# Down projections of a decoder layer's two feed-forward blocks: features 8 to 21 by seven half-size products for each pair of output tiles

## The chip, the cores and the metric

The kernel runs on one core of one Trainium2 chip. The metric is the device time of one execution in microseconds (us). An engine is named as in the profile: PE is the matrix engine (TensorE), PEld its weight load, DVE the vector engine, ACT the scalar engine, POOL the GpSimd engine, SP the engine that mostly issues DMAs.

## The reference

One layer on 512 rows of 1024 values, all float32. The part that matters here is the feed-forward block, which stands at the start and at the end of the layer:

```python
D_FF = ((8 * D_MODEL // 3 + 127) // 128) * 128      # 2816 = 22 x 128

def swiglu(h, w_gate, w_up, w_down):
    return (jax.nn.silu(h @ w_gate) * (h @ w_up)) @ w_down

x = x + 0.5 * swiglu(rms_norm(x, norm_ffn1[l]), w1_gate[l], w1_up[l], w1_down[l])
# two token mixers, then the cross-attention
x = x + 0.5 * swiglu(rms_norm(x, norm_ffn2[l]), w2_gate[l], w2_up[l], w2_down[l])
return rms_norm(x, norm_final)
```

The change touches the last product of each block, `... @ w_down`: 2816 features in, 1024 values out, for 512 rows.

## The kernel before

The activations are held transposed: a tile has 128 features in its partitions and the 512 rows in its columns. So `x` is 8 tiles of 128x512, and the result of the gate and up projections, `act`, is 22 tiles of 128x512 ("features 0 to 21" below means these 22 tiles).

Every product in float32 is made of three matmuls in a format of less precision (`fp32r`). An operand `v` is split into `h` (ACT rounds it into `fp32r`) and `l = v - h` (DVE subtracts), and the product is `h*h + h*l + l*h`. `split` does this, and `wload` does it for a piece of weights: SP loads it (`wr`, three buffers), ACT writes `wh`, DVE writes `wl` (two buffers each).

The down projection of a block is the second half of the function `ffn`. It makes 8 output tiles. An output tile takes 22 features x 3 matmuls, each with a stationary 128x128 piece of weights and a moving 128x512 piece of `act`. The weights of an output tile come in three chunks of 8, 8 and 6 features (`DOWN`). The first two output tiles are computed together, chunk by chunk (line 553); tiles 2 to 7 go one after the other through `dense` (line 130). When a tile is done, DVE adds it to `x` (line 532), and `nrm.feed` adds its squares to the sum of the next norm (`acc`, line 188). In the second block the last tile is computed in two halves of 256 columns (again line 130), so that the end of the kernel (transposes, `finish`, line 1287; the output's scaling, lines 1305 and 1306; the output's DMAs, lines 1308 to 1311) can begin on the first half.

The gate and up projections ahead of it are already made by seven products of half-size blocks in place of eight: pairs of feature tiles, columns 0 to 255 and 256 to 511 as the two halves, with operand sums and result sums on DVE and ACT. Their recorded operations all have line 78. There a product has moving pieces of 128x256 or 128x512.

In the first block a `hook` makes tables for the mixers between the tiles of the down projection: at tile 3 four small matmuls (line 644) make a position table from a one-hot matrix `oh`, DVE copies them out (`fab`, line 646), POOL sends them to DRAM (line 647), and POOL then issues 16 DMAs that spread them (line 651).

The order on each engine comes from a scheduler with priorities, save where `ordered()` or `high_priority` holds an instruction. An engine runs its instructions in that order, and each waits for what it reads and for the buffer that it writes.

## Time and profile before

| | us |
|---|---|
| time, median of 3 runs | 1260.16 (1260.11 to 1261.1) |
| the profiled execution: time | 1260.48 |
| the profiled execution: span from first to last instruction | 1258.5 |
| down projection of the first block, on PE | 232.40 to 357.98 |
| down projection of the second block, on PE | 1121.89 to 1249.65 |

The span is the time between the first and the last instruction in the trace, so 1.98 us of the profiled time lie outside it. "Busy" sums overlapping instructions only once. Matmuls are pipelined: one shows a duration of 0.28 or 0.39 us, but the next starts sooner, and what counts is the distance between starts (the pitch). All positions are microseconds from the start of the span.

### The profile page before, as it was taken

What the parts mean: (1) busy time and instruction counts of PE and PEld (TensorE: products, weight loads), DVE (VectorE), ACT (ScalarE), POOL (GpSimd) and SP (SyncE); (2) the same over time, 40 slices, a digit from 0 to 9 for tenths busy, and PEclk for the clock granted to TensorE, in tenths of its full rate; (3) what the DMA queues carried; (4) which work ended last, traced back from release to release, by engine and by line L of the source; (5) the groups of instructions that cost most, each with busy time, mean ns of one, the idle gap of its engine ahead of it and who ended that gap; (6) DMA issues with size and microseconds to landing.
All of it is one profiled execution on the core that took longest, in us unless ns stands there. A gap on an engine that the chain in (4) does not pass through costs nothing.

```text
span 1258.5 us, 17814 instructions
## 1 busy us (share of the span) xinstructions
PE 1247.4 (99%) x6517; PEld 1052.5 (84%) x6517; DVE 895.6 (71%) x1842; ACT 704.7 (56%) x1424; POOL 74.8 (6%) x101
## 2 busy tenths in 40 slices
PE   9999999999999999999999999999999999999997
PEld 7888888887888788888888898887888888888887
DVE  5899888844356988887878666555689888884224
ACT  5466666732244777777774554444547666672223
POOL 1001111003000000000001000000001111000000
PEclk9999999999999999999999999999999999999999
DMA  6738776238443522221224345212446777723233
GB/s 222 192 101 192 194 188 175 79 117 257 149 139 101 184 66 96 71 77 55 84 89 156 112 134 184 84 51 67 124 136 175 192 193 179 182 73 104 84 101 113
DMA packets 58791, 165.93 MB, mean 132 GB/s; under 512 B 6248, under 2 KB 6512, under 8 KB 58704
## 3 DMA queue, kind: packets, MB, share of 16 engines
q1 hardware_dynamic: 44096, 129.16, 32.0%
q0 software_dynamic: 14032, 34.57, 12.8%
q8 instruction: 51, 0.84, 0.3%
q10 hardware_dynamic: 576, 1.07, 0.2%
q14 instruction: 36, 0.29, 0.1%
HBM read 160.54 MB, written 10.07 MB: 136 GB/s over the span
## 4 chain that ended last, share of the span: by engine, by line
PE 95%; DVE 3%; ACT 1%; DMA 1%; issue 0%; DVEq 0%; SPq 0%; ACTq 0%
PE ps_d L130 44%; PE ps_d L78 12%; PE ps_t L78 8%; PE ps_d L553 5%; PE ps_s L78 5%; PE ps_o L78 4%; PE ps_d L1044 4%; PE ps_d L1198 2%; PE ps_t L929 1%; PE ps_s L842 1%; PE ps_o L837 1%; PE ps_s L841 1%; PE ps_o L836 1%; PE ps_d L792 1%; PE ps_o L1257 1%; PE ps_s L1231 1%
## 5 line engine op out<-in xcount | busy, mean ns | idle before, releaser
L105 ACT ACTIVATE wh<-wr 128x512 fp32r<-128x512 f32 (+3 forms) x255 | 167.5, 690 | 302.2 <-PE ps_d L130 160.0
L106 DVE TENSOR_TENSOR wl<-wr,wh 128x512 fp32r<-128x512 f32 (+3 forms) x255 | 189.6, 769 | 142.1 <-ACT wh L105 140.2
L130 PE MATMUL ps_d<-xh,wl 128*128 128x512 f32 x424 | 169.8, 400 | 0.0
L130 PE MATMUL ps_d<-xh,wh 128*128 128x512 f32 x424 | 168.6, 398 | 0.0
L130 PE MATMUL ps_d<-xl,wh 128*128 128x512 f32 x424 | 168.4, 397 | 0.0
L130 PEld LDWEIGHTS ps_d<-xh,wl 128*128 128x128 f32 x424 | 79.7, 188 | 16.5 <-DVE wl L106 0.5
L130 PEld LDWEIGHTS ps_d<-xl,wh 128*128 128x128 f32 x424 | 79.7, 188 | 15.9
L130 PEld LDWEIGHTS ps_d<-xh,wh 128*128 128x128 f32 x424 | 79.8, 188 | 15.6
L130 PE MATMUL ps_d<-al,wh 128*128 128x512 f32 (+1 forms) x195 | 73.9, 379 | 0.0
L130 PE MATMUL ps_d<-ah,wh 128*128 128x512 f32 (+1 forms) x195 | 73.9, 379 | 0.0
L130 PE MATMUL ps_d<-ah,wl 128*128 128x512 f32 (+1 forms) x195 | 73.8, 378 | 0.0
L78 DVE TENSOR_TENSOR wl<-wr,wh 128x1024 fp32r<-128x1024 f32 (+1 forms) x49 | 52.1, 1071 | 20.9 <-ACT wh L78 20.8
L130 PE MATMUL ps_d<-ahl,wh 128*128 128x512 f32 (+1 forms) x182 | 53.1, 376 | 0.0
L78 PE MATMUL ps_o<-t,h2h 128*128 128x256 f32 x272 | 50.4, 283 | 0.0
L78 DVE TENSOR_TENSOR h2l<-s,h2h 128x512 fp32r<-128x512 f32 x68 | 44.1, 688 | 8.4 <-ACT h2h L78 8.0
L78 PE MATMUL ps_d<-n,h2h 128*128 128x512 f32 x136 | 49.9, 401 | 0.0
L78 PE MATMUL ps_d<-t,h4h 128*128 128x512 f32 x136 | 49.6, 399 | 0.0
L78 PE MATMUL ps_t<-b,h5h 128*128 128x512 f32 x136 | 49.4, 397 | 0.0
L78 PE MATMUL ps_t<-n,h3h 128*128 128x512 f32 x136 | 49.3, 395 | 0.0
L78 PE MATMUL ps_s<-b,wh 128*128 128x512 f32 x136 | 49.1, 395 | 0.0
L78 PE MATMUL ps_d<-b,wh 128*128 128x512 f32 x136 | 49.0, 393 | 0.0
L78 ACT ACTIVATE wh<-wr 128x1024 fp32r<-128x1024 f32 (+1 forms) x49 | 45.2, 931 | 6.8 <-DMA wr<-in_w_first_dram 3.6
(387 smaller groups left out, 3306.3 us busy)
## 6 DMA issues: line engine op xcount, KB each, us to landing
wr<-in_w_down_dram SPq DMA_DIRECT2D x34, 512.0 KB, 3.5
wr<-in_w_in_dram SPq DMA_DIRECT2D x29, 512.0 KB, 3.5
wr<-in_w_gate_dram SPq DMA_DIRECT2D x25, 512.0 KB, 4.9
wr<-in_w_up_dram SPq DMA_DIRECT2D x25, 512.0 KB, 5.1
s<-in_w_gate_dram SPq DMA_DIRECT2D x17, 512.0 KB, 4.5
s<-in_w_gate_dram POOLq DMA_DIRECT2D x17, 512.0 KB, 6.0
s<-in_w_up_dram SPq DMA_DIRECT2D x17, 512.0 KB, 4.2
s<-in_w_up_dram POOLq DMA_DIRECT2D x17, 512.0 KB, 6.5
```

The lines of the kernel that those rows point to most:

```text
L78: return lambda *args, **kw: tc.keep_in_program_order(call(*args, **kw))
L105: A.activation(h, src, AF.Copy)
L106: V.tensor_sub(l, src, f32(h))
L130: yield T.matmul(out, w[:, c], m, start=i == 0, stop=i == total - 1)
L553: T.matmul(two[m], w[:, cc], v, start=f == 0 and z == 0, stop=f == FT - 1 and z == 2)
L792: T.matmul(pv[i][:, :VC], m[k][:, tk], ww[:, w], start=k == 0 and z == 0, stop=k == KT - 1 and z == 2)
L836: T.matmul(po[:, cols], w, h[:, src], start=start, stop=False, skip_group_check=True)
L837: T.matmul(po[:, cols], w, l[:, src], start=False, stop=False, skip_group_check=True)
L841: first = T.matmul(out, q[:, tk], kk[0][:, ks], start=True, stop=False)
L842: T.matmul(out, q[:, tk], kk[1][:, ks], start=False, stop=True)
L1044: yield T.matmul(pj, w[:, c], m, start=n == 0, stop=n == 11)
L1198: T.matmul(pj[t], m[k][:, tk], ww[:, w], start=k == 0 and z == 0, stop=k == KT - 1 and z == 2)
```

## The change

`ffn` is cut into `gate_up` and `down`, with memory pools of their own. In `down`, features 0 to 7 (`NA`) are multiplied as before, for all 8 output tiles. Features 8 to 21 are taken as two halves, 8 to 14 and 15 to 21 (`ND` = 7 tiles each). With two output tiles and the two halves of the columns, this is a product of 2x2 blocks, and it is made by seven products of blocks in place of eight, for each of four pairs of output tiles. One product is 7 features x 3 matmuls with a moving piece of 128x256.

The sums of blocks of `act` (`nt`, `nt2`) and their splits (`b11`, `nh` and `nl`, `bh` and `bl`) are made by `prepare_top` and `prepare_bottom`; the sums of blocks of the weights are made by a DMA that adds (`load_s`: SP loads one half twice, POOL adds the other) and by DVE (`s2`). `ready(i)` makes the weights of product `i`, two products ahead. `results` copies a partial sum on ACT or adds a finished one to `x` on DVE, 256 columns at a time. The tables are made ahead of tile 4 in place of tile 3 (`HOOK` = 3, called with `m - 1`), in four pieces, in buffers shared with the block operands. The end of the second block is written anew for the new order of its results (`part`, `turn`, `sums`, `leave`), with as many transposes and output DMAs as before. The diff, cut to its core:

```diff
-DOWN = (8, 8, 6)
+NA = 8
+ND = (FT - NA) // 2
+WD = ND * P
+NK = 22
...
+HOOK = 3
+BOTTOM = {0: (2,), 1: (3, 4), 2: (5, 6)}
+TOPS = (2, 1, 1, 1, 1, 1)
...
-                    ahead.append(down_weights(q + 1 - NQ, 0))
+                    ahead.append(wload(a[f"w{tag}_down"][q + 1 - NQ][:, :NA * P], NA * P))
...
+        def load_s(q):
+            q_[q]["s"] = t = pool.tile([P, 2, WD], F32, tag="S", name="s31", bufs=2)
+            o = src[2 * q + 1]
+            SY.dma_start(t, bass.AP(o.tensor, o.offset + NA * P, [[FF, P], [0, 2], [1, WD]]))
+            o = src[2 * q]
+            G.dma_start(t, bass.AP(o.tensor, o.offset + NA * P, [[FF, P], [P * FF + WD, 2], [1, WD]]),
+                        accum_op=ALU.add)
...
+        def prepare_top(k):
+            t, b = act[NA + k], act[NA + ND + k]
+            ta, tb_, ba, bb = t[:, :256], t[:, 256:], b[:, :256], b[:, 256:]
+            nt, nt2 = ext("nt"), ext("nt2")
+            V.tensor_sub(nt[:, :256], ta, tb_)
+            V.tensor_sub(nt[:, 256:], bb, tb_)
+            V.scalar_tensor_tensor(nt2[:, :256], nt[:, :256], -1.0, bb, op0=ALU.mult, op1=ALU.subtract)
+            V.scalar_tensor_tensor(nt2[:, 256:], nt2[:, :256], -1.0, ba, op0=ALU.mult, op1=ALU.subtract)
+            b11 = block("b11")
+            blk["b11"][k] = b11[:, :256], b11[:, 256:]
+            split(*blk["b11"][k], ta)
+            for n1, n2, v in (("n1", "t3", nt), ("n2", "t4", nt2)):
+                h, l = block("nh"), block("nl")
+                split(h, l, v)
+                blk[n1][k] = h[:, :256], l[:, :256]
+                blk[n2][k] = h[:, 256:], l[:, 256:]
+
+        def prepare_bottom(k):
+            h, l = block("bh"), block("bl")
+            split(h, l, act[NA + ND + k])
+            blk["b21"][k] = h[:, :256], l[:, :256]
+            blk["b22"][k] = h[:, 256:], l[:, 256:]
...
+        for f in range(NA):
+            if ah[f] is None:
+                act_split(f)
...
+        seq = []
+        NQ = KT // 2
+        for q in range(NQ):
+            seq += [("1", q), ("7", q)]
+            if q:
+                seq.append(("4", q - 1))
+            if last and q == NQ - 1:
+                seq += [("6", q), ("2", q), ("4", q), ("3", q - 1), ("5", q), ("3", q)]
+                break
+            seq += [("6", q), ("2", q)]
+            if q:
+                seq.append(("3", q - 1))
+            seq.append(("5", q))
+            if q == NQ - 1:
+                seq += [("4", q), ("3", q)]
+        used = {"1": "b11", "7": "t3", "6": "n2", "2": "b21", "5": "n1", "4": "t4", "3": "b22"}
+        def ready(i):
...
+            if p == "7":
+                d["s2"] = pool.tile([P, WD], F32, tag="s2", name="s2", bufs=2)
+                V.tensor_add(d["s2"], d["s"][:, 1], d["r11"])
+            raw = {"1": "r11", "2": "r12", "4": "r22", "3": "s2", "6": "s2"}.get(p)
+            raw = d[raw] if raw else d["s"][:, 0 if p == "7" else 1]
+            if last and i == len(seq) - 1:
+                t = pool.tile([P, 2, WD], F32R, tag="S", name="ws", bufs=2)
+                ws[i] = t[:, 0], t[:, 1]
+            elif i % 3 == 1:
+                ws[i] = tuple(pool.tile([P, WD], F32R, tag="w3" + z, name="w3", bufs=1) for z in "hl")
+            else:
+                ws[i] = tuple(t[:, :WD] for t in wpair())
+            split(*ws[i], raw)
+            if p == ("2" if last and q == NQ - 1 else "5"):
+                V.tensor_add(d["s2"], d["s2"], d["r12"])
+            n = {"7": "r11", "5": "r12", "4": "r22"}.get(p)
+            if n and q + 1 < NQ:
+                load(q + 1, n)
+            if p == "5" and q + 2 < NQ:
+                load_s(q + 2)
+        tops = list(range(ND))
+        for m in range(2, KT):
+            if hook:
+                hook(m - 1)
+            pd = bank("d")
+            dense(pd, [(src[m][:, :NA * P], NA)], ah, al, step=1024)
+            if m < KT - 1:
+                update(m, pd)
+            else:
+                with ordered():
+                    for n in ("r11", "r12", "r22"):
+                        load(0, n)
+                    with tc.high_priority(offset=AHEADF):
+                        ready(0)
+                        ready(1)
+                    update(m, pd)
+            for _ in range(TOPS[m - 2]):
+                prepare_top(tops.pop(0))
+        for k in range(2):
+            prepare_bottom(k)
+
+        def product(out, w, n, start=False):
+            for k in range(ND):
+                c = slice(k * P, (k + 1) * P)
+                h, l = blk[n][k]
+                for i, (ww, m) in enumerate(((w[0], h), (w[0], l), (w[1], h))):
+                    T.matmul(out, ww[:, c], m, start=start and k + i == 0, stop=k == ND - 1 and i == 2,
+                             skip_group_check=True)
...
+        def results(i):
...
+            if p == "1":
+                d["ga"] = bank("s")
+                A.activation(d["ga"][:, :256], d["x"][:, :256], AF.Copy)
+            elif p == "6":
+                d["gb"] = bank("t")
+                A.activation(d["gb"][:, :256], d["x"][:, :256], AF.Copy)
+            elif p == "7":
+                late.append(lambda: add7(m + 1, d["p7"]))
+            elif p == "2":
+                add(m, 0, d["ga"], 1)
...
+        def seven():
...
+                d = q_[q]
+                for k in BOTTOM.get(i, ()):
+                    prepare_bottom(k)
+                if not (last and i == len(seq) - 3):
+                    ready(i + 2)
...
+            for n in "sstt":
+                t = bank(n)
+                T.matmul(t[:, :256], ah[0][:, :P], al[0][:, :256], start=True, stop=True, skip_group_check=True)
+            seven()
...
-        TB = ((0, 1024, "h2h"), (1024, FA + FB - 1024, "h2l"))
+        TB = ((0, 512), (512, 512), (1024, FA - 1024), (FA, FB))
...
-            if m != 3:
+                return
+            if m != HOOK:
                 return
...
-                        fab = pool.tile([P, S], F32, tag="E", name="fab", bufs=NE)
-                        V.tensor_copy(fab[:8, :e1 - e0], b[:8, :e1 - e0])
-                        nc.gpsimd.dma_start(dst[:, e0 - lo:e1 - lo], fab[:8, :e1 - e0])
...
+                fab = pool.tile([P, S], F32, tag="E", name="fab", bufs=4)
+                V.tensor_copy(fab[:8, :n], b[:8, :n])
+                nc.gpsimd.dma_start(dst[:, c0 - lo:c0 - lo + n], fab[:8, :n])
```

How the order of instructions changes is shown at two places. First PE in the first block. Before, in the middle of an output tile (here tile 4, `ps_d`), features 0 to 7 (`ah`, `al`) were followed by features 8 and on (`ahl`):

```order
L130 MATMUL ps_d_3060<-ah_2704,wh_3093 128x512
L130 MATMUL ps_d_3060<-al_2705,wh_3093 128x512
L130 MATMUL ps_d_3060<-ah_2704,wl_3094 128x512
L130 MATMUL ps_d_3060<-ahl_2708,wh_3093 128x512 x2
L130 MATMUL ps_d_3060<-ahl_2708,wl_3094 128x512
L130 MATMUL ps_d_3060<-ahl_2775,wh_3123 128x512 x2
L130 MATMUL ps_d_3060<-ahl_2775,wl_3124 128x512
```

Now all 8 output tiles end with feature 7; after the last (tile 7) come four matmuls into unused banks, and then the first two of 28 products (operands `b11` and `nh`, `nl`; weights `wh`, `wl` and `w3`):

```order
L136 MATMUL ps_d_2990<-ah_2624,wh_2993 128x512
L136 MATMUL ps_d_2990<-al_2625,wh_2993 128x512
L136 MATMUL ps_d_2990<-ah_2624,wl_2994 128x512
L84 MATMUL ps_s_3065<-al_841,ah_840 128x256
L84 MATMUL ps_s_3067<-al_841,ah_840 128x256
L84 MATMUL ps_t_3069<-al_841,ah_840 128x256
L84 MATMUL ps_t_3071<-al_841,ah_840 128x256
L84 MATMUL ps_d_3081<-b11_2718,wh_3027 128x256 x2
L84 MATMUL ps_d_3081<-b11_2718,wl_3028 128x256
```

In place of 42 matmuls of 512 columns for features 8 to 21 in each tile, PE has 147 matmuls of 256 columns for each pair of tiles, behind all the others.

The second place is DVE in the same block. Before, between the additions of two finished tiles to `x` (tiles 4 and 5), it had the splits of three chunks of weights (`wl`), one step of the norm and one split for the next stage (`xl`):

```order
L532 SCALAR_TENSOR_TENSOR x4_65<-ps_d_3060,x4_65 128x512
L106 TENSOR_TENSOR wl_3183<-wr_3180,wh_3182 128x1024
L188 TENSOR_TENSOR acc_2832<-acc_2832,sq_3146 128x512
L234 SCALAR_TENSOR_TENSOR xl4_3433<-x4_65,gains_69,xh4_3432 128x512
L106 TENSOR_TENSOR wl_3213<-wr_3210,wh_3212 128x768
L106 TENSOR_TENSOR wl_3242<-wr_3239,wh_3241 128x1024
L532 SCALAR_TENSOR_TENSOR x5_66<-ps_d_3149,x5_66 128x512
```

Now, from the addition of the last tile on (`x7`, features 0 to 7 only), the splits of block operands stand between the splits of weights; `wl_3078` is for the third product (number 6), `wl_3114` for the fourth, `w3_3148` for the fifth:

```order
L84 SCALAR_TENSOR_TENSOR x7_68<-ps_d_2990,x7_68 128x512
L112 TENSOR_TENSOR nl_3054<-nt2_3041,nh_3053 128x512
L112 TENSOR_TENSOR bl_3058<-act_1901,bh_3057 128x512
L112 TENSOR_TENSOR bl_3062<-act_2091,bh_3061 128x512
L84 TENSOR_TENSOR bl_3074<-act_2129,bh_3073 128x512
L84 TENSOR_TENSOR wl_3078<-s2_3031,wh_3077 128x896
L84 TENSOR_TENSOR bl_3106<-act_2316,bh_3105 128x512
L84 TENSOR_TENSOR bl_3110<-act_2354,bh_3109 128x512
L84 TENSOR_TENSOR wl_3114<-wr_3023,wh_3113 128x896
L84 TENSOR_TENSOR bl_3140<-act_2520,bh_3139 128x512
L84 TENSOR_TENSOR bl_3144<-act_2555,bh_3143 128x512
L84 TENSOR_TENSOR w3_3148<-s31_2606,w3_3147 128x896
```

The norm's steps and the splits `xl` have moved behind, into the products; the work on block operands is new at this place.

## Rows read from the trace of the kernel before

**Rows 1.** The page: the span, the busy time of the engines (share of the span, number of instructions), and the shares of the chain of work that ended last.

```profile
span 1258.5 us, 17814 instructions
...
PE 1247.4 (99%) x6517; PEld 1052.5 (84%) x6517; DVE 895.6 (71%) x1842; ACT 704.7 (56%) x1424; POOL 74.8 (6%) x101
...
PE 95%; DVE 3%; ACT 1%; DMA 1%; issue 0%; DVEq 0%; SPq 0%; ACTq 0%
```

**Rows 2.** Windows: start and end of a stretch and its length; then PE, PEld, DVE, ACT and POOL busy (number of instructions); the granted clock of PE, the DMAs' share and GB/s. The stretches are the end of the gate and up projections of the first block, two parts of its down projection, the gate and up projections of the second block, and two parts of its down projection.

```profile
76.00:232.40 156.40, 156.32 (x951) 139.39 (x952) 139.18 (x252) 108.10 (x210) 16.46 (x15) 1.00 0.67 175
232.40:279.00 46.60, 46.60 (x204) 37.40 (x203) 25.44 (x42) 19.47 (x34) 1.10 (x2) 1.00 0.33 102
279.00:358.00 79.00, 79.00 (x341) 62.98 (x340) 28.98 (x37) 20.92 (x28) 13.05 (x25) 1.00 0.59 189
...
945.00:1122.00 177.00, 176.80 (x1072) 157.31 (x1073) 157.14 (x283) 119.61 (x234) 17.70 (x15) 1.00 0.67 171
1122.00:1167.00 45.00, 45.00 (x198) 36.43 (x197) 23.58 (x40) 19.40 (x34) 0.00 (x0) 1.00 0.31 94
1167.00:1249.80 82.80, 82.80 (x441) 70.63 (x440) 29.34 (x43) 25.96 (x38) 0.00 (x0) 1.00 0.31 98
```

**Rows 3.** Timeline of PE at the start and the end of the first block's down projection, and at the start of the second's: start, duration, operation, output from inputs, shape.

```profile
232.40 0.39 PE L553 MATMUL ps_d<-ah,wh 128*128 128x512 f32 x1
...
357.98 0.40 PE L130 MATMUL ps_d<-xh,wh 128*128 128x512 f32 x1
...
1121.89 0.39 PE L553 MATMUL ps_d<-ah,wh 128*128 128x512 f32 x1
```

**Rows 4.** The chain of waits, in order of time: start, length, what, and the number of instructions in the piece. The first is a product of the gate and up projections with 256 columns; the others are pieces of the down projections, the second of them the leftover of the stage before.

```profile
104.45 1.44 PE ps_o L78 x12
...
233.72 1.55 PE ps_t L78 x8
...
286.27 74.67 PE ps_d L130 x320
...
1242.34 7.47 PE ps_d L130 x62
```

**Rows 5.** Timeline of PE in the last output tile of the second block: the first matmul of its first half (66 matmuls of 256 columns), the last, and the transposes behind.

```profile
1232.20 0.28 PE L130 MATMUL ps_d<-ah,wh 128*128 128x256 f32 x1
...
1239.91 0.28 PE L130 MATMUL ps_d<-ahl,wl 128*128 128x256 f32 x1
1240.04 0.82 PE L1287 MATMUL ps_d<-ident,gx 128*128 128x128 f32 x6
```

**Rows 6.** Groups of instructions of one line and shape, from 1228 to 1250 us: PE's weight loads for matmuls of 256 columns: number, busy us, mean ns of one, idle us before them.

```profile
L130 PEld LDWEIGHTS ps_d<-ah,wh 128*128 128x128 f32 x30 | 5.7, 188 | 0.0
```

**Rows 7.** The same view for DVE and ACT: four shapes on DVE over the whole span, the addition to `x` and a 256-column operation between 76 and 360 us, and two shapes on ACT.

```profile
L106 DVE TENSOR_TENSOR wl<-wr,wh 128x1024 fp32r<-128x1024 f32 x38 | 46.5, 1225 | 49.2 <-ACT wh L105 49.1
L106 DVE TENSOR_TENSOR wl<-wr,wh 128x768 fp32r<-128x768 f32 x11 | 10.5, 958 | 35.2 <-ACT wh L105 35.2
L532 DVE SCALAR_TENSOR_TENSOR x<-ps_d,x 128x512 f32<-128x512 f32 x8 | 5.5, 692 | 16.9 <-PE ps_d L130 13.0 <-PE ps_d L553 3.9
L78 DVE TENSOR_TENSOR act<-act,sg 128x256 f32<-128x256 f32 x16 | 6.8, 425 | 0.5
L105 ACT ACTIVATE wh<-wr 128x512 fp32r<-128x512 f32 x196 | 114.6, 623 | 148.1 <-PE ps_d L130 74.2 <-issue 27.2 <-PE ps_d L553 19.8
L105 ACT ACTIVATE wh<-wr 128x1024 fp32r<-128x1024 f32 x38 | 40.3, 1060 | 114.5 <-PE ps_d L130 82.5 <-issue 20.6 <-PE ps_d L553 6.4
```

**Rows 8.** Timeline of DVE at the start of the first block's down projection, for the distance between starts: 256 columns (the first three), 512 columns (the last two).

```profile
232.60 0.42 DVE L78 TENSOR_TENSOR act<-ps_t,p 128x256 f32<-128x256 f32 x1
233.06 0.42 DVE L78 TENSOR_TENSOR act<-ps_t,act 128x256 f32<-128x256 f32 x1
233.40 0.41 DVE L78 TENSOR_TENSOR act<-ps_d,p 128x256 f32<-128x256 f32 x1
...
238.33 0.69 DVE L106 TENSOR_TENSOR al<-act,ah 128x512 fp32r<-128x512 f32 x1
238.93 0.69 DVE L106 TENSOR_TENSOR ahl<-act,ahl 128x512 fp32r<-128x512 f32 x1
```

**Rows 9.** DMA issues: number, KB each, median us from issue to landing.

```profile
wr<-in_w_down_dram SPq DMA_DIRECT2D x34, 512.0 KB, 3.5
s<-in_w_gate_dram SPq DMA_DIRECT2D x17, 512.0 KB, 4.5
s<-in_w_gate_dram POOLq DMA_DIRECT2D x17, 512.0 KB, 6.0
s<-in_w_up_dram POOLq DMA_DIRECT2D x17, 512.0 KB, 6.5
fa_r<-fa_d POOLq DMA_DIRECT2D x8, 520.0 KB, 11.9
fa_d<-fab POOLq DMA_DIRECT2D x2, 16.0 KB, 2.7
```

**Rows 10.** Timeline of the end of the kernel: the last matmul, the addition of the last half tile to `x`, and the first scaling of the last output rows.

```profile
1249.53 0.28 PE L130 MATMUL ps_d<-ahl,wl 128*128 128x256 f32 x1
...
1249.85 0.42 DVE L565 SCALAR_TENSOR_TENSOR x<-ps_d,x 128x256 f32<-128x256 f32 x1 [2.06 <-PE ps_d L130]
...
1252.64 0.69 ACT L1305 ACTIVATE out<-ps_o,nr 128x512 f32<-128x512 f32 x1 [0.82 <-DVE nr L214]
```

## The prediction

> **What bounds the kernel now.** I read the page first: of a span of 1258.5 us PE is busy for 1247.4, and the chain of work that ended last is PE for 95% [rows 1]. The reader is to see that the time is a count of matmuls times their pitch. Then the windows by stage: in both down projections PE is busy in every microsecond at a granted clock of 1.00, while DVE is busy 25.4 of the first 46.6 us and 29.0 of the next 79 us of the first block, and much the same in the second [rows 2]. So in these two stages a matmul less is time less, as long as DVE, ACT and the DMAs keep up; and DVE has room, though not without end: in the gate and up projections it is busy 139.4 of 156.4 us, and PE still has no gap there [rows 2]. The down projection of the first block runs on PE from 232.40 to 357.98 us, where the next stage's first matmul starts without a gap [rows 3]: 125.6 us. The second's runs from 1121.89 us [rows 3] to the last matmul's end at 1249.53 + 0.12 = 1249.65 us [rows 10]: 127.8 us.

> **The pitches.** A matmul of 512 columns: 320 of them in 74.67 us of the chain, 0.2333 us each [rows 4]. A matmul of 256 columns: 12 in 1.44 us, 0.120 [rows 4]; 66 without any other between 1232.20 and 1240.04 us, 0.1188 [rows 5]; 62 in 7.47 us at the end, 0.1205, among a few others [rows 4]. I take 0.1195 with ends of 0.1188 and 0.1205. Half the columns cost 0.512 of the whole, so the seven-for-eight saving survives nearly unhurt.

> The rule that speaks against this: each of these matmuls has a weight load of its own, which shows 188 ns [rows 6], more than the pitch of 120 ns, but it lies beside other matmuls and weight loads, since 66 in a row kept 0.1188. [...]

> **The change, part by part.** Removed, in each block: features 8 to 21, that is 8 tiles x 14 x 3 = 336 matmuls of 512 columns. Added: 4 pairs x 7 products x 7 x 3 = 588 matmuls of 256, and 4 more into unused banks.

> First block: 336 x 0.2333 = 78.39 us go, 592 x 0.1195 = 70.74 come: -7.65 us. The four small table matmuls stay, and so does the leftover of the stage before, 1.55 us [rows 4]. Second block: there the last tile already ran in halves. 7 tiles x 42 = 294 matmuls of 512 go, and 84 of 256. The pitch of 512 is a little shorter in this block: from 1121.89 to 1232.20 us [rows 3, 5] lie 462 of them, the leftover of about 1.5 us and 16 transposes of about 0.12, which gives (110.3 - 1.5 - 1.9)/462 = 0.2314. So 68.0 + 84 x 0.1195 = 78.1 go, 70.7 come, and the first features of the last tile go back from 48 x 0.1195 to 24 x 0.2314 (-0.2): -7.5 us. Together -15.2 us. The ends of the narrow pitch move this by 1184 x 0.0007 = 0.8 down or 1184 x 0.001 = 1.2 up.

> Behind the last matmul nothing should change: adding the last half tile to `x` starts 0.3 us after it began, and the first output scaling 2.8 us later [rows 10]; the new end has the same half tile, sums, transposes and output DMAs. I cost it at 0, from -0.5 to +1.5: before, 66 matmuls (7.9 us) [rows 5] and more lay between the ends of the two halves of the rows, now one product (2.5 us), so the output DMAs of the first half lie closer to those of the second.

> What must be hidden is DVE's and ACT's work in the first 46 us, and this is where I expect a small loss. PE takes 192 x 0.2333 + about 2.5 us (leftover and tables) + 0.5 from 232.40 until the products start: 280.2 us. The first three products (2.5 us each) put the start of the third, number 6, at 285.2. DVE must by then have done 76 instructions, counted in its new order from 238.93 us, where before it began the splits of features 8 and on [rows 8]. Of 256 columns: 28 sums of blocks and 7 splits, at a pitch of 0.34 where the operands are old [rows 8] and up to 0.43, a whole duration [rows 7], where each waits for the one before (21 can): 35 x 0.34 = 11.9 to 13.8. Of 512: 17 splits at 0.60 [rows 8], 10.2, and 8 additions to `x` at 0.60 to 0.69 [rows 7], 5.2. Of 1024: 6 splits at 1.225 [rows 7] less the 0.09 by which neighbours overlap, 6.8. Of 896 columns, which this trace doesn't have: 4, between 0.958 and 1.225 [rows 7], nearer the latter, 1.09 less 0.09: 4.0. The tables: 1.7. Sum 39.8 to 41.7, so ready at 279 to 281 if DVE never waits. But it runs in order, and two waits stand in the way: the addition of tile 3 stands ahead of the table copies and waits for PE (some 2 us), and the next sum of blocks (`nt`) takes the buffer of a table copy whose DMA needs 2.7 us to land [rows 9] (some 1 to 2). That gives 282 to 285 against 285.2. The margin is 0 to 3 us. Queued behind these waits are the splits of weights for tiles 5 to 7 and the first products, and PE waits for those. I take a loss of 0.8 us for the first block, from 0 to 5. In the second there are no tables, and I take 0, up to 2.

> ACT has 14 `nh`, 7 `b11`, 3 `bh` and 4 splits of weights more in that stretch: 17 x 0.62 + 7 x 0.40 + 4 x 0.95 = 17 us beside the 19.5 it has, less the splits of features 8 to 21 that go: below 37 of 47 us [rows 2, 7]. It hides.

> In the products a pair lasts 147 x 0.1195 = 17.6 us. DVE has 7 splits and 2 sums of 896 (9 x 1.0), one addition of 512 and four of 256 (0.7 + 4 x 0.4), two norm steps (2 x 0.6) and, in the first block, two splits for the next stage (2 x 0.7): about 13.9 us, 79%, where the gate and up projections run 89% [rows 2]. The weights of a product are split two products ahead, 5 us, against about 2.0 for one split on ACT and DVE. A pair's weights are 3.2 MB of reads, 182 GB/s; the gate and up stages move 171 to 175 without a gap on PE [rows 2]. The adding DMA takes 6.0 to 6.5 us to land [rows 9] and is issued more than a pair ahead; in the first block it shares POOL's queue with the 16 table DMAs, which land in 11.9 us [rows 9]. I cost this at 0, from 0 to 3.

> Sum against the profiled execution: 1260.48 - 15.2 + 0.8 = 1246.1; that execution is 0.3 us above the median. I predict 1246 us. Its own range is 1243.8 to 1249.

> **The rivals.**

> *PE waits at the joint.* DVE's queue is late by more than the margin in the first block, and a little in the second, so that PE stands still ahead of the first products: 3 to 9 us together. For it: the waits above, and a stage that goes from 55% DVE [rows 2] to about 95%. Against it: PE's gap-free gate and up stage at 89%. Time 1249 to 1255, point 1251. Chance 0.18.

> *Products held by their own operands (slower).* Place: every product. If the lead of two products is used up by DVE's in-order queue (an addition to `x` that waits for PE stands ahead of a split that PE waits for), each product waits for its split. 56 products lose the gain of 15.2 us when each waits 0.27; half of a 896 split on DVE (0.55 us) each is 56 x 0.55 = 31 us, 1276. For it: 9 splits and sums in line with 5 additions per pair. Against: 21% of DVE's time free and 5 us of lead. Chance 0.07.

> *The gain is given back, no change.* The adding DMAs come late behind the table DMAs, one pair waits for a landing of 12 us in the first block, and the end gains nothing: about 1260. That the gate and up stages move 171 to 175 GB/s with adding DMAs of the same kind and no gap [rows 2, 9] is against it. Chance 0.03.

> *Narrow matmuls paced by their weight loads (slower).* At 0.188 us [rows 6] for each of 1176 the change costs 1176 x 0.188 - 2 x 78.3 = +65 us, 1325; it decides from a pitch of 156.5/1176 = 0.133. The 66 in a row at 0.1188 speak against it [rows 5]. [...] Chance 0.02.

> **How the numbers follow.** The forecast's own range gets 0.67; 0.03 is left for below 1243.8, if the narrow pitch is at its low end and nothing waits. The range of 8 in 10 takes in the joint's waits: 1243.5 to 1254. About 0.2% (2.5 us) is what a measurement of this kernel can tell from no change. Faster: 0.67 + 0.18 + 0.03 = 0.88; same 0.03; slower 0.07 + 0.02 = 0.09.

> **What would show it.** The products' rows should have a pitch of 0.119 to 0.121 us, and each block's down projection should last 118 to 120 us on PE. If I am right about the joint, idle time ahead of PE's weight loads is below 2 us, released by DVE `wl` or `w3` around product 6 of the first block. Steps gone wrong would be: idle time of PE ahead of every product (second rival), a releaser among DMAs in the first block (third), a pitch above 0.125 (last), or more than 10 us between the last matmul's start and the span's end.

## The result, and the profile after

The change takes 1245.7 us (median of 4 runs, 1245.47 to 1246.24) against 1260.6 us (median of 4, 1260.11 to 1261.1) before: a ratio of 0.9882 with a 95% interval of 0.9865 to 0.99. That is 14.9 us less, and the spans of the profiled executions differ by as much, 1258.5 and 1243.6.

The page after, its span, engines and chain, as in [rows 1]:

```profile
span 1243.6 us, 18977 instructions
...
PE 1232.5 (99%) x6979; PEld 1066.1 (86%) x6979; DVE 978.5 (79%) x1990; ACT 740.0 (60%) x1478; POOL 85.6 (7%) x111
...
PE 95%; DVE 3%; ACT 1%; DMA 1%; issue 0%; ACTq 0%; SPq 0%; DVEq 0%
```

PE has 462 instructions more and 14.9 us less of work, DVE 83 us more, and the bound is still PE. The windows by stage, as in [rows 2] (stretch, length, PE, PEld, DVE, ACT, POOL, clock, DMA share, GB/s): first part and products of the first block, gate and up projections and what lies around them, first part and products of the second block.

```profile
232.40:280.00 47.60, 47.60 (x211) 38.06 (x210) 43.22 (x85) 24.24 (x43) 15.58 (x27) 1.00 0.83 260
280.00:349.30 69.30, 69.30 (x591) 69.30 (x590) 56.47 (x76) 39.29 (x57) 7.95 (x12) 1.00 0.66 190
349.30:1113.10 763.80, 761.39 (x4061) 645.77 (x4060) 586.87 (x1323) 466.68 (x1014) 37.54 (x47) 1.00 0.41 121
1113.10:1159.80 46.70, 46.70 (x206) 37.67 (x205) 43.36 (x83) 26.02 (x42) 2.36 (x2) 1.00 0.59 169
1159.80:1234.10 74.30, 74.30 (x631) 74.30 (x630) 51.66 (x74) 37.66 (x56) 2.36 (x2) 1.00 0.38 106
```

PE has no gap in any of the four stretches that the change touches, at a granted clock of 1.00. DVE in the first 47 us went from 25.4 to 43.2 us of work [rows 2], and still nothing waits. The timeline of PE gives the bounds of the stages, as in [rows 3]:

```profile
232.50 0.39 PE L606 MATMUL ps_d<-ah,wh 128*128 128x512 f32 x1
...
279.96 0.40 PE L84 MATMUL ps_d<-b,wh 128*128 128x256 f32 x2
...
349.28 0.39 PE L136 MATMUL ps_d<-xh,wh 128*128 128x512 f32 x1
...
1112.90 0.39 PE L606 MATMUL ps_d<-ah,wh 128*128 128x512 f32 x1
```

| us | before | after | difference | predicted |
|---|---|---|---|---|
| down projection, first block | 125.58 | 116.78 | -8.8 | -6.85 |
| between the two | 763.91 | 763.62 | -0.3 | 0 |
| down projection, second block | 127.76 | 121.23 | -6.5 | -7.5 |
| last matmul's start to the end | 8.97 | 9.59 | +0.6 | 0 |

At the joint, the timelines of PE and of its weight loads, and of DVE, around product 6:

```profile
284.80 0.29 PE L84 MATMUL ps_o<-nh,w 128*128 128x256 f32 x1
284.92 0.28 PE L84 MATMUL ps_d<-nh,wh 128*128 128x256 f32 x1
```

```profile
285.04 0.19 PEld L84 LDWEIGHTS ps_d<-nh,wl 128*128 128x128 f32 x1
```

```profile
282.10 0.69 DVE L84 TENSOR_TENSOR bl<-act,bh 128x512 fp32r<-128x512 f32 x1
282.70 1.08 DVE L84 TENSOR_TENSOR wl<-s,wh 128x896 fp32r<-128x896 f32 x1
```

Product 6 starts at 284.92. Its `wl` is finished at 282.70 + 1.08 = 283.78 and first loaded at 285.04: a margin of 1.3 us.

### The profile page after: what moved, and what is told of

Read it like the earlier page. It is cut to its first block, busy times and chain, and to the rows that moved or that the text cites. A ratio compares the mean times of both kernels' runs of the same rounds, so it can differ in the third digit from the quotient of the medians.

```text
span 1243.6 us, 18977 instructions
## 1 busy us (share of the span) xinstructions
PE 1232.5 (99%) x6979; PEld 1066.1 (86%) x6979; DVE 978.5 (79%) x1990; ACT 740.0 (60%) x1478; POOL 85.6 (7%) x111
## 4 chain that ended last, share of the span: by engine, by line
PE 95%; DVE 3%; ACT 1%; DMA 1%; issue 0%; ACTq 0%; SPq 0%; DVEq 0%
PE ps_d L136 36%; PE ps_d L84 17%; PE ps_t L84 11%; PE ps_s L84 6%; PE ps_o L84 6%; PE ps_d L1306 4%; PE ps_d L1460 2%; PE ps_d L606 2%; PE ps_t L1191 1%; PE ps_s L1104 1%; PE ps_o L1099 1%; PE ps_s L1103 1%; PE ps_o L1098 1%; PE ps_d L1054 1%; PE ps_o L1519 1%; PE ps_s L1493 1%
## 5 line engine op out<-in xcount | busy, mean ns | idle before, releaser
L111 ACT ACTIVATE wh<-wr 128x512 fp32r<-128x512 f32 (+1 forms) x206 | 132.7, 679 | 151.4 <-PE ps_d L136 69.6
L112 DVE TENSOR_TENSOR wl<-wr,wh 128x512 fp32r<-128x512 f32 (+1 forms) x206 | 150.0, 754 | 31.8 <-ACT wh L111 29.8
L136 PEld LDWEIGHTS ps_d<-xh,wl 128*128 128x128 f32 x424 | 79.8, 188 | 16.5 <-DVE wl L112 0.5
L84 DVE TENSOR_TENSOR wl<-wr,wh 128x1024 fp32r<-128x1024 f32 (+2 forms) x67 | 71.7, 1075 | 24.6 <-ACT wh L84 24.2
L84 ACT ACTIVATE wh<-wr 128x1024 fp32r<-128x1024 f32 (+2 forms) x67 | 62.3, 935 | 17.7 <-PE ps_o L84 4.6
L84 PE MATMUL ps_d<-b,wh 128*128 128x512 f32 (+1 forms) x220 | 64.2, 351 | 0.0
L84 DVE TENSOR_TENSOR s<-s,wr 128x512 f32<-128x512 f32 (+1 forms) x84 | 63.9, 760 | 0.0
L84 PE MATMUL ps_d<-b,wl 128*128 128x256 f32 x178 | 50.1, 281 | 0.6 <-DVE wl L84 0.6
L84 POOL DMA_DIRECT2D s<-in_w_gate_dram x17 | 20.1, 1182 | 357.2 <-DMA s<-in_w_gate_dram 286.6
L84 ACT ACTIVATE h2h<-s 128x512 fp32r<-128x512 f32 x68 | 39.1, 623 | 8.8 <-DVE s L84 8.8
```

The source lines that it names most:

```text
L84: return lambda *args, **kw: tc.keep_in_program_order(call(*args, **kw))
L111: A.activation(h, src, AF.Copy)
L112: V.tensor_sub(l, src, f32(h))
L136: yield T.matmul(out, w[:, c], m, start=i == 0, stop=i == total - 1)
```

## Experiments

**One block alone.** The second block's down projection and the end are those of before (the old function, called for that block):

```diff
+    def ffn_old(pool, tag, nrm_in, gin, nrm, gi, first=None, hook=None, done=None):
```

> The first block as changed, the second block's down projection and end as before. My theory (matmul count times pitch, block by block): the trace of the change has the first block's down projection 8.8 us shorter and the second's 6.5 us shorter with an end 0.6 us longer, so this kernel should be 8.8 us faster than before, about 1251.8, with 0.3 either way. Rival (part of the gain lies in the second block's new end or in the split of the pools, not in the products): the first block alone would give clearly less, 7 us or below.

Measured: 1252.2 us (1251.99 to 1252.32), ratio 0.9933 (0.9916 to 0.9949). The first block's stage lasts 116.78 us as in the change, the second's 127.75 as before. So the first block's gain does not need the second's change. It is 8.8 us by the stage and 8.5 by the time (the end came out 0.4 us longer here): larger than the 6.85 I had forecast for it, with the second's smaller.

**The lead of the operands.** `ready(i)` makes the weights of product i on ACT and DVE; the change calls it two products ahead.

```diff
-                        ready(1)
...
-                if not (last and i == len(seq) - 3):
-                    ready(i + 2)
-                if last and i == len(seq) - 5:
-                    ready(i + 4)
+                ready(i + 1)
```

> As changed, but the weights of a product are made one product ahead, not two. My theory: a split takes about 2.0 us on ACT and DVE (3.0 with a sum ahead of it) against 2.5 us for a product, so some products now wait a few tenths: +2 to +10 us, and the idle time of PE is released by DVE wl or w3. Rival (products are never near to waiting, the lead is worthless): 0 within 1 us. Rival (even now each product is held by its operands): +50 us or more.

With `ready(i)` right ahead of the product instead:

> As changed, but the weights of a product are made right ahead of it in the program's order, behind the addition of the product before on DVE. My theory: where such an addition stands ahead (some 40 of 56 products), PE waits for the addition (0.4), the split on DVE (1.0) and where there is one the sum (1.0): 1.5 to 2.5 us each, +60 to +100 us. Rival (the order of DVE does not matter since it has 20% of its time free): below +10 us.

Measured, one run each: 1249.9 us with a lead of one (4.2 above the change; the first stage 1.3 and the second 2.3 us longer), and 1361.2 with none (115 above it; the stages 46 and 65 us longer). The second figure is beyond what I expected. The windows of the products without a lead:

```profile
279.90:392.00 112.10, 76.98 (x550) 70.56 (x548) 54.14 (x70) 35.46 (x51) 7.41 (x11) 0.95 0.40 111
1208.00:1347.00 139.00, 97.26 (x631) 89.62 (x630) 55.07 (x76) 38.20 (x57) 2.36 (x2) 0.87 0.23 64
```

PE stands idle for 35 of 112 us and 42 of 139, and the granted clock has a mean of 0.95 and 0.87. Part of the matmuls are slower too: from 288.35 to 291.12 us they start 0.213 us apart in place of 0.118. How the excess divides between waiting and slower matmuls was not measured apart. A product that waits for its own operands loses 46/28 = 1.6 us in the first block, the slower matmuls included, not the 0.55 that my second rival gave it. The lead of two is what keeps that rival out; one product is nearly enough.

**Narrow matmuls.** The second block's products as two matmuls of 128 columns, 1176 of them:

```diff
+                    for z in ((0, 128, 256) if last else (0, 256)), :
+                        for z0, z1 in zip(z, z[1:]):
+                            T.matmul(out[:, z0:z1], ww[:, c], m[:, z0:z1], start=start and k + i + z0 == 0,
```

> As changed, but in the second block each matmul of a product is made as two of 128 columns, 1176 in place of 588. If columns alone set the pitch (half of 0.119 us each), nothing changes: 0 to +2 us. If a matmul cannot come sooner than its weight load allows, the transposes of 128 columns in the traces (0.109 us from start to start) are the floor: 1176 x 0.109 = 128 us in place of 70, +58 us. I lean to the second: 256 columns would then lie just above the floor.

Measured, in one run: 1307.1 us, 61.4 above the change. Two pieces of the chain of waits of this kernel (start, length, what, instructions), and the row of one group of its weight loads (number, busy us, mean ns of one, idle us before them):

```profile
1174.10 4.69 PE ps_s L84 x42
...
1192.86 9.38 PE ps_d L84 x84
```

```profile
L84 PEld LDWEIGHTS ps_d<-nh,wl 128*128 128x128 f32 x84 | 12.8, 192 | 0.0
```

Half the columns again cost 0.1117 us, not 0.06. The 192 ns that a weight load lasts are not the pace, since a matmul with one of its own follows every 112 ns. The sums of squares at the end of the change, of a single column, come every 0.111 us (8 in 0.89 us, in the rows further down). So 256 columns at 0.118, 128 at 0.1117 and one at 0.111 us lie close together. Why was not tested; the weight loads, one for each matmul, come at the same distance (from 1160 to 1296 us 1220 of them beside 1222 matmuls, both busy for all of the 136 us). By these figures a further halving by narrower tiles has little left to give here.

**How much more DVE the joint takes.** Three, six and twelve additions of 512 columns, into a tile that nothing reads, are put in DVE's queue ahead of the first products' operands in the first block:

```diff
+                    if hook:
+                        for _ in range(3):
+                            V.tensor_add(idle, act[NA + ND], act[NA + ND])
```

> As changed, with 3 more DVE additions of 512 columns (about 0.62 us each, 1.9 us in all) in the first block, ahead of the splits for the first product; their result is not used. In the trace of the change the split for the third product (number 6) ends 1.14 us before PE needs it. My theory: 1.1 us are free, the rest is paid in full: PE waits 0.7 to 0.9 us there. Rival A (PE already waits for DVE at this place): 1.9 us. Rival B (later slack takes it up): 0.

> The same with 6 additions, about 3.7 us. My theory: 2.5 to 2.7 us of waits. Rival A: 3.7. Rival B: 0.

> The same with 12 additions, about 7.4 us. My theory: 6.2 to 6.4 us of waits, the first of them at the first product (its split has 3.8 us to spare). Rival A: 7.4. Rival B: below 3.

The first stage became 0.9, 2.2 and 9.4 us longer (1246.9, 1248.1 and 1254.6 us in all, one run each). The first agrees with the margin: with three additions, 1.8 us of DVE, the split for product 6 ends at 286.02, 2.2 us later than in the change, which is 0.9 more than the margin. From 284.92 to 286.31, around the start of product 6, PE needs 1.39 us for four matmuls, 0.9 more than at 0.118 each. One wait there, of 0.36 us, is long enough to be listed, and there is none anywhere else in this stage:

```profile
284.92 0.28 PE L84 MATMUL ps_o<-nh,w 128*128 128x256 f32 x1
285.22 0.38 PE L84 MATMUL ps_d<-nh,wh 128*128 128x256 f32 x1
...
286.08 0.39 PE L84 MATMUL ps_d<-nh,wl 128*128 128x256 f32 x1 [0.36 <-DVE wl L84]
286.31 0.28 PE L84 MATMUL ps_d<-nh,wh 128*128 128x256 f32 x1
```

The second is a little under what I expected, and the third misses it by 3 us. There the scheduler also set eight operations on block operands, which the change runs later, ahead of the first product's split. That split ends at 285.85 + 1.09 = 286.94 us, 10.8 later than in the change, of which the additions are 7.2. So PE waits at the first product and not at product 6, 7.1 us in all, nearer to rival A's 7.4 than to my 6.2 to 6.4; this run does not measure the margin. Its timeline (DVE, then PE) and two windows:

```profile
285.85 1.09 DVE L84 TENSOR_TENSOR wl<-wr,wh 128x896 fp32r<-128x896 f32 x1
```

```profile
287.00 0.58 PE L84 MATMUL ps_d<-b,wl 128*128 128x256 f32 x1 [6.98 <-DVE wl L84]
287.38 0.63 PE L84 MATMUL ps_d<-b,wh 128*128 128x256 f32 x2
287.80 0.41 PE L84 MATMUL ps_d<-b,wl 128*128 128x256 f32 x1
```

```profile
287.00:290.00 3.00, 3.00 (x14) 3.00 (x15) 3.00 (x4) 0.95 (x1) 0.00 (x0) 0.50 0.62 115
290.00:300.00 10.00, 10.00 (x79) 10.00 (x79) 8.09 (x12) 6.32 (x10) 0.00 (x0) 0.91 0.16 46
```

After 7 us without a matmul the granted clock is 0.50 from 287 to 290 us, and the next 23 matmuls, nearly all 0.213 us apart in place of 0.118, take 5.0 us in place of 2.7: 2.3 us on top of 7.1 of waits, together 9.4. So this wait had a second price, and my 1251 for the first rival lacked it.

**Where the pitches come from.** In the second block's down projection of before, two pitches of 512 columns stand side by side (PE timeline of before):

```profile
1226.97 0.40 PE L130 MATMUL ps_d<-al,wh 128*128 128x512 f32 x1
1227.20 0.40 PE L130 MATMUL ps_d<-ah,wl 128*128 128x512 f32 x1
1227.44 0.62 PE L130 MATMUL ps_d<-ahl,wh 128*128 128x512 f32 x2
```

Those with `al` and `ah` start 0.23 us apart. The 21 with `ahl` last from 1227.44 to 1232.20 [rows 5], 0.2267 us each. The same 21 of the first block's last tile last from 353.08 to 357.98 [rows 3], 0.2333:

```profile
353.08 0.63 PE L130 MATMUL ps_d<-ahl,wh 128*128 128x512 f32 x2
```

Clock (granted 1.00 in both stretches [rows 2]), shape and type are equal. What differs is the operands' address in SBUF, which the traces do not show and which I took from the built program: `ahl` lies 32 bytes further on in the first block (165312 against 165280 in each partition). Two simple theories first. One: the moving tiles are best at an odd multiple of 32, as the weights `wh` and `wl` are; two spare tiles of 32 bytes move them there.

```diff
+    g.tile([P, 8], F32, name="pad0", bufs=1)
...
+    g.tile([P, 8], F32, name="pad1", bufs=1)
```

> As changed, with two spare tiles of 32 bytes per partition, so that the tiles of x, its splits and act (moving operands) lie 32 bytes past a multiple of 64, as the weights wh and wl already do; the block operands of the down projections stay where they are. In the traces 512-column matmuls start every 0.2333 us where the moving tile lies on a multiple of 64 and the weights do not, and every 0.227 us where both lie 32 past one (ahl of the second block before). Theory (the places of the two operands set the pitch): some 2400 of the 512-column matmuls gain 0.006 us each: 10 to 16 us faster than the change, 1230 to 1236. Rival (the 0.227 has another cause, such as less DMA traffic in the second block): no change within 1 us.

Measured: 1244.9 us (1244.56 to 1245.49), ratio to before 0.9874 (0.9857 to 0.989). The theory fell: 512 columns stayed at 0.233 (the 131 ahead of the first block's down projection took 30.59 us, 0.2335 each). The second theory: the weights at a multiple of 128 bytes, by 96 and 32 spare bytes, in the change and in the kernel before:

```diff
+    g.tile([P, 24], F32, name="pad1", bufs=1)
...
+            padded.append(g.tile([P, 8], F32, name="pad2", bufs=1))
```

> As changed, with 96 spare bytes per partition ahead of the tiles wh and wl, so that they lie on a multiple of 128 bytes, as the tiles of x, its splits and act do already (before: wh and wl 32 past one). The run with both moved to 32 past a multiple of 64 showed no gain, so that theory has fallen; the rows of three traces sorted anew say: 512-column matmuls whose two operands lie at the same distance from a multiple of 128 bytes start every 227 to 229 ns, all others every 233. New theory: some 1650 of them in stages of 512 columns alone gain 5 us per 1000, while 256-column ones at the same distance lose 1 ns each and the gate and up stage 2 us: 5 to 8 us faster than the change, 1238 to 1241. Rival (the 227 comes from something else): no change within 1 us.

> The kernel before with the same spare bytes. New theory: about 2200 matmuls of 512 columns gain 5 ns each, the gate and up stage loses 2 us: 7 to 11 us faster than before, 1249 to 1253. Rival: no change within 1 us.

Measured: 1245.9 us with a ratio of 0.9881 (0.9867 to 0.9896), and 1260.6 with 0.9998 (0.9988 to 1.0007). No change in either; this theory fell too.

Then I took the pitch of each matmul of 512 columns in six traces by the distance between its two operands' addresses, these again from the built programs. At a multiple of 256 bytes the mean was 0.229 us, at nearly all other distances 0.232 to 0.233. In the trace of before alone, of the matmuls of 512 columns behind which another of 512 follows, the 253 at a multiple of 256 bytes have a median of 0.227 us and a mean of 0.228, the 2644 at other distances a mean of 0.233. In the kernel before, `ahl` and `wh` are 161 x 256 apart in the second block. The next kernel puts the weights behind the `x` and `act` tiles, in tiles of 4224 bytes:

```diff
+        h, l = (g.tile([P, 1056], F32R, tag="wh", name="wh", bufs=2)[:, off:off + 1024],
+                g.tile([P, 1056], F32R, tag="wl", name="wl", bufs=2)[:, off:off + 1024])
```

> As changed, with places chosen by stage: weights at the same distance as the moving tile for 512 columns, 64 bytes apart in the products of the down projections (in the traces 256-column matmuls start every 116.6 to 117.2 ns there, 118.3 or 119.6 at other distances), and as now in the gate and up stage. New theory: 9 to 13 us faster than the change, 1233 to 1237. Rival: no change within 1 us.

Measured: 1241.2 us (1240.37 to 1241.39), ratio 0.9845 (0.9829 to 0.9862), half of what I expected. 4224 is 16.5 x 256, so only every other buffer came to a multiple of 256 bytes. One stretch of 131 matmuls of 512 columns, ahead of the first block's down projection, shows what that gave. In the built program 59 of these lie at a multiple and 72 are 128 off, and the piece of the chain reads:

```profile
32.36 30.23 PE ps_d L137 x131
```

That is 0.2308 us each. In the change, where none of the 131 lies at a multiple, it is 0.2334, and in the next kernel, where all do, 0.2270 (both further down). With tiles of 4096 bytes nearly all of the kernel's matmuls of 512 columns lie at a multiple; the products' weights alone, whose matmuls have 256 columns, are set 64 bytes off (three more spare tiles, not shown, keep the operands in the pools of the down projections in step):

```diff
-    def wpair():
-        return (g.tile([P, 1024], F32R, tag="wh", name="wh", bufs=2),
-                g.tile([P, 1024], F32R, tag="wl", name="wl", bufs=2))
+    def wpair(off=0):
+        h, l = (g.tile([P, 1024], F32R, tag="wh", name="wh", bufs=2)[:, off:],
+                g.tile([P, 1024], F32R, tag="wl", name="wl", bufs=2)[:, off:])
+        return h, l
...
     x = [big(F32, f"x{k}") for k in range(KT)]
+    wpair()
...
+                ws[i] = tuple(t[:, :WD] for t in wpair(16))
```

> As changed, with the four tiles wh and wl moved right behind the tiles of x, its splits and act, so that all lie at the same distance from a multiple of 256 bytes; the weights of the products 64 bytes apart from their moving tiles as in the run before (there the tiles of wh and wl were 4224 bytes long, so that only every other one lay at that distance). The rows of six traces by the distance of the two operands: 229 ns at 0 and at 256 bytes modulo 512, 232 to 233 ns at nearly all others, 128 and 384 among them. Theory (the distance modulo 256 decides for 512 columns): the first 192 matmuls of each down projection take 46.4 us or less (46.8 to 47.5 as changed), and the kernel is 8 to 12 us faster than the change, 1234 to 1238, though the gate and up stage may lose 2 us. Rival (distance alone does not decide, as modulo 128 did not): no faster than the run before it, 1240 or more.

Measured: 1236.2 us (1235.84 to 1236.82), a ratio to before of 0.9807 (0.9791 to 0.9823): 9.5 us below the change and the fastest kernel of the study. The chain of waits, first of the change, then of this kernel; the two pieces are the same stretches of 131 and 164 matmuls of 512 columns in both, the first ahead of the first block's down projection, the second between the two down projections:

```profile
32.91 30.57 PE ps_d L136 x131
...
896.57 38.27 PE ps_d L136 x164
```

```profile
32.32 29.74 PE ps_d L137 x131
...
890.66 37.22 PE ps_d L137 x164
```

The pitch went from 0.2334 to 0.2270 in both, with a granted clock of 1.00 from 33 to 63 us in either kernel. Its windows, for the first part and the products of the second block:

```profile
1105.90:1151.40 45.50, 45.50 (x207) 37.65 (x206) 43.06 (x83) 25.92 (x43) 2.37 (x2) 1.00 0.61 172
1151.40:1224.96 73.56, 73.56 (x633) 73.56 (x631) 51.59 (x74) 37.82 (x56) 2.36 (x2) 1.00 0.39 108
```

The granted clock is 1.00 here as it is in the change. The first part, nearly all of 512 columns, takes 45.5 us, with 46.8 in the change, whose products start at 1159.66; the products take 73.6 for 74.5. Of the 9.1 us between the two spans, 4.7 lie between the down projections, which the change does not touch. The distance for 512 columns was found in six traces and then foretold this one (1234 to 1238 us expected, 1236.2 measured). Why the distance matters stays open, and so does the best distance for 256 columns: the 64 bytes were not tried by themselves. Nor was the placement tried on the kernel before.

## Why the prediction was right

The time came within 0.3 us (1246 against 1245.7), by the mechanism forecast: a PE without gaps, and fewer columns to multiply. Point by point:

*The bound.* Right. PE is busy in all four stretches, and a wait showed there only where an edit made one (a lead cut short, DVE work added). The sign that I gave was too narrow, though: I wanted 118 to 120 us for each down projection, and they took 116.8 and 121.2. And the 139.4 us that I gave for DVE in the gate and up projections are the weight loads' figure in that row; DVE's is 139.2, also 89% [rows 2].

*The narrow pitch.* Taken as 0.1195, it is (349.28 - 279.96)/588 = 0.1179 in the first block, below the low end of 0.1188, and 0.1191 in the second. In the first block 592 x 0.0016 = 0.95 us: with the joint's loss that did not come (0.8) this is 1.75 of the 1.95 us by which the first block beat its forecast.

*The wide pitch of the second block.* I took one mean of 0.2314 for all that goes. It was two pitches, and half of the 294 matmuls removed were the short ones (147 with `ahl`). The mean cost little: added up from the distances between PE's starts, the block has 62.4 us less of 512-column matmuls, against 62.5 by my mean.

*Sums and transposes.* Here a step failed: "the new end has the same half tile, sums, transposes". For each half of the rows PE now has 16 matmuls that sum squares where it had 8. The transposes are 32 in both kernels, but 26 of them lie before the last product's end where 24 did. So 42 small matmuls lie there in place of 32; added up from PE's starts they take 4.5 us in place of 3.2. These 1.3 us, which I had put at nothing, are more than the 1.0 us that the second block's gain lacks; the pitch of the narrow matmuls gave the difference back. The other sums lie in the end, the timeline of which reads (as [rows 10]):

```profile
1234.01 0.29 PE L84 MATMUL ps_t<-bh,ws 128*128 128x256 f32 x1
...
1234.33 0.42 DVE L84 SCALAR_TENSOR_TENSOR x<-ps_t,x 128x256 f32<-128x256 f32 x1 [1.00 <-PE ps_t L84]
...
1234.50 1.03 PE L84 MATMUL ps_o<-ones,sq 128*128 128x1 f32 x8
1235.39 0.31 PE L84 MATMUL ps_t<-ident,x 128*128 128x128 f32 x1
...
1235.86 0.50 PE L84 MATMUL ps_o<-ones,sq 128*128 128x1 f32 x4
```

Before, the last sums began 1.23 us after the last matmul's end (1250.88), now 1.73 (1235.86 - 1234.13): 0.5 of the 0.6 us by which the end is longer, inside the range of -0.5 to +1.5 that I had given.

*The joint.* The place, the releaser and the margin were right: I had the weights of product 6 ready at 282 to 285 against 285.2, they were at 283.8, and three more additions on DVE brought a wait there. The loss of 0.8 us was a mean over that margin; what came was 0. How DVE came to 283.8 was in part luck. Of the two waits that I put at 3 to 4 us in all, the addition of tile 3 waits 1.30 us for PE, and no `nt` waits for a table copy; the other 2.9 us of DVE's waits are six shorter ones, for PE and ACT, that I had not named:

```profile
256.56 0.69 DVE L589 SCALAR_TENSOR_TENSOR x<-ps_d,x 128x512 f32<-128x512 f32 x1 [1.30 <-PE ps_d L136]
...
260.33 0.55 DVE L908 COPY fab<-ps_t 8x384 f32<-8x384 f32 x1 [0.69 <-PE ps_t L906]
260.81 0.40 DVE L566 TENSOR_TENSOR nt<-act 128x256 f32<-128x256 f32 x1
```

The price of an 896-column operation, 1.09 with a pitch of 1.00, was met:

```profile
275.03 1.09 DVE L84 TENSOR_TENSOR wl<-wr,wh 128x896 fp32r<-128x896 f32 x1
276.03 1.08 DVE L84 TENSOR_TENSOR s<-s,wr 128x896 f32<-128x896 f32 x1
277.03 1.08 DVE L84 TENSOR_TENSOR w<-s,w 128x896 fp32r<-128x896 f32 x1
```

*DVE in the products, and the DMAs.* DVE is busy 56.5 of 69.3 us, 81% (79 forecast). An adding DMA of 896 KB took 9.5 us to land, longer than the 6.0 to 6.5 us that I took from 512 KB, but it is issued more than a pair, 17 us, ahead (after; number, KB each, median us from issue to landing):

```profile
s<-in_w_down_dram SPq DMA_DIRECT2D x8, 896.0 KB, 5.5
s<-in_w_down_dram POOLq DMA_DIRECT2D x8, 896.0 KB, 9.5
fa_r<-fa_d POOLq DMA_DIRECT2D x8, 520.0 KB, 11.2
```

*The rivals.* The first was near: 1.3 us of margin. The second needs a lead under one product: without any, the kernel took 115 us more, not 31, part of it in matmuls 0.213 us apart. The third did not happen, and the last is excluded by the pitch itself, 0.118 and 0.119 us, though 128 columns came every 0.1117 us and not in half of that, which was not in my account.

So that the total was met to 0.3 us is luck in part, since errors cancel: the first block gave 1.95 us more than forecast, the second block and the end 1.6 less.

## What to carry to other kernels

Where an engine has no gap, price a change in instructions times pitch, but read the pitch for each pair of operands apart and count the small instructions around the moved work too. Before trusting a hidden cost, compute when its last product is ready against when it is needed, and test that margin by adding work: here a lead of one product less cost 4 us, and of two less 115. When such a test is built, look where the scheduler put the added work: with 12 additions it had reordered the rest. Where matmuls of one shape show two pitches at one clock (here 0.227 and 0.233 us at 1.00), compare the operands' addresses too.
